# One region of nested arms per expert in a streamed mixture-of-experts loop

## The chip, the cores and the metric

The kernel runs on one core of a Trainium2 chip. The metric is the device time of one execution in microseconds (us), lower is better. A core has five engines that run their own instruction streams and meet through semaphores: TensorE (PE in the profile, with its weight loads as PEld), VectorE (DVE), ScalarE (ACT), GpSimd (POOL) and SyncE (SP). A name with a q (PEldq, ACTq) is the sequencer of that engine: it runs branches, register and semaphore instructions and hands the rest on.

## What is computed

The reference is two post-norm layers of a diffusion backbone over 1024 latent tokens and 256 context tokens, model width 1024, float32. Each layer has a mixing half (attention, pooling, a convolution module, one output projection) and then a hierarchical mixture of experts: each token picks one of four groups and the two best of the eight experts in it, and each expert is a SwiGLU of inner width 512. Cut to what matters here:

```python
def expert_block(args):                     # one block of 128 tokens of one expert
    tb, e = args
    xb = h[tb]
    return (jax.nn.silu(xb @ wg[e]) * (xb @ wu[e])) @ wd[e]
ys = lax.map(expert_block, (tok_buf.reshape(nblk, MOE_BLOCK), blk_e))
return jnp.zeros_like(h).at[tok_buf].add(ys.reshape(P, D) * w_buf[:, None])
```

The router decides at run time how many tokens each of the 32 experts of a layer gets. With the routing that these inputs give, over both layers, 37 experts have at most 64 tokens, 17 have 65 to 128, and 10 have more than 128 (nine of these 129 to 256, one 385 to 448).

## The kernel before

**Stages.** In the profiled execution the mixing half of layer 0 runs to 857 us, its experts from 857 to 1652 us, the mixing half of layer 1 to 2386 us, its experts from 2386 to 3145 us, and a final combination to the end.

**The loop.** `moe` goes over the 32 experts in a Python loop, so each expert has its own code in the program; nothing is reused from one expert to the next. The weights of an expert are 6.29 MB of float32. `e_loads` streams them by SyncE through a ring of 14 units of 1 MiB, six per expert: units 0 to 3 hold gate and up, 4 and 5 the down projection. `load_n` (L2230) reads into registers of every engine the number n of 64-token pieces of an expert, three experts ahead.

**An expert.** `gather` (L2049) fetches up to 128 token rows by an indirect DMA of GpSimd, two experts ahead. `xt_pe` (L2059) transposes them on TensorE in two groups of four, and `xt_copy` brings them to `xT` (ScalarE L2064, VectorE L2065). Then come gate and up:

- `half` (L2092), for at most 64 tokens: 16 matmuls of 64 columns in plain float32 straight from the ring;
- `full`, for more: every product is made of three matmuls of rounded parts (L172 to L174). Weights and tokens must be split first, by `ws` and `xs`: ScalarE makes the high part (`wh`, `xh`, L167), VectorE the rest (`wl`, `xl`, L168). `full` makes the last splits itself; the first, three of weights and two of tokens, are `prep(e)`, made ahead.

`act` (L2140 on ScalarE, L2141 on VectorE) computes silu(gate) times up in two halves `sg`, `ht` (L2147 on TensorE, L2148 on ScalarE) transposes each half into `g`, `down` (L2158) multiplies with the down weights into `mpy`, `evac` (L2163, L2164) copies that to `my`, and `scatter` (L2172) writes the rows out by indirect DMAs.

**The order of an expert.** All of it is written out by hand; each engine runs in program order, and every engine runs every branch. A first nest of `tc.If` (L2264, L2267, L2268) chooses gate and up; then common code follows (the loads, the copies `pl`, the conditional gather `over` of the rows beyond 128 of the expert three ahead, `act`, `xt_pe` of the next expert, `ht`, `xt_copy`); a second nest (L2298, L2301, L2303, L2309) chooses the down projection and, for more than 128 tokens, the second chunk's `act`, `ht` and `down`; then `prep` of the next expert under a branch of its own (L2321), `evac`, loads and `scatter`. The true part of an `If` lies first in the program, its else part behind it, so an expert of over 64 tokens jumps over the code of `half` at L2264, and one of at most 64 tokens jumps, at the end of `half`, over all the code for more. On TensorE this last jump (also L2264) passes 1370 instructions, the one at L2267 1270 and the one at L2298 163.

## Time and profile before

| | us |
|---|---|
| median of 3 runs | 3215.35 |
| lowest, highest | 3204.18, 3216.85 |
| the profiled execution's own time | 3213.33 |
| its span in the trace | 3211.5 |
| experts of layer 0 (857 to 1652 us) | 795 |
| experts of layer 1 (2386 to 3145 us) | 759 |

The profiled execution lies 2 us under the median, and its trace covers all but 1.8 us of it. The change touches only the two expert stages, together 1554 us, so everything is read there. Times in the rows are us unless marked ns. "Idle before" and "waits" name what ended an engine's idle time; "issue" is time in which the engine waited for nothing that the profile shows, as when its sequencer had no instruction to give it. The records of a sequencer's own instructions have a duration too, and for a branch this holds the time until the next instruction is there.

### The profile page before, as it was taken

How to read it: one execution, taken by the hardware profiler on the slowest of the kernel's cores; microseconds unless marked ns; L12 is line 12 of the kernel's file. 1: busy time of each engine (PE TensorE's matmuls, PEld its weight loads, DVE VectorE, ACT ScalarE, POOL GpSimd, SP SyncE). 2: the span in 40 equal slices, each digit the busy share in tenths (PEclk: the TensorE clock that was granted, in tenths of full speed). 3: DMA queues.
4: the chain of work that ended last, by engine and by line, in shares of the span. 5: the costliest groups of instructions: out<-in, count | busy, mean ns of one | idle time of the engine just before them, and what ended most of it. 6: DMA issues, size and time to landing. Idle time of an engine off the chain costs nothing. (4 is left out here: it accounts for less than half of the span.)

```text
span 3211.5 us, 41598 instructions
## 1 busy us (share of the span) xinstructions
PE 2635.0 (82%) x13118; PEld 1663.1 (52%) x13118; DVE 1493.3 (46%) x2851; ACT 1188.0 (37%) x2260; POOL 1070.6 (33%) x919
## 2 busy tenths in 40 slices
PE   6988899998488769879757989999957788798783
PEld 4766565576254435455227766666732344554331
DVE  3355556487543323334149555556851332333215
ACT  3223666632143323333135337665211322333212
POOL 1023999223311121211136349941331111111114
PEclk8998999999799889999878999999978899899997
DMA  7542000042778685757976530002279876645995
GB/s 270 215 142 74 1 1 1 1 158 85 277 297 335 231 310 184 278 188 264 360 295 193 183 136 1 1 1 96 88 260 380 312 288 248 233 158 203 340 361 230
DMA packets 280605, 616.63 MB, mean 192 GB/s; under 512 B 63376, under 2 KB 77072, under 8 KB 271504
## 3 DMA queue, kind: packets, MB, share of 16 engines
q1 hardware_dynamic: 251696, 562.24, 47.9%
q0 software_dynamic: 24544, 37.91, 3.4%
q10 hardware_dynamic: 3712, 8.88, 0.7%
q8 instruction: 275, 4.51, 0.6%
q14 instruction: 378, 3.10, 0.3%
HBM read 577.09 MB, written 73.81 MB: 203 GB/s over the span
## 5 line engine op out<-in xcount | busy, mean ns | idle before, releaser
L1327 DVE TENSOR_REDUCE mx<-S 128x1 f32<-128x1024 f32 (+1 forms) x272 | 215.3, 798 | 208.9 <-PE S L1322 208.5
L172 PE MATMUL gu<-wh,xh 128*128 128x512 f32 x432 | 188.8, 437 | 119.2 <-issue 100.5
L2158 PE MATMUL mpy<-er,g 128*128 128x512 f32 (+1 forms) x672 | 242.8, 630 | 9.9 <-issue 7.3
L2172 POOL DMA_INDIRECT y_d<-my,pl x128 | 140.8, 1100 | 321.5 <-ACTq L2264 108.8
L1339 ACT ACTIVATE P<-S,nb 128x256 f32<-128x256 f32 (+1 forms) x272 | 208.6, 773 | 33.7 <-DVE nb L1331 32.6
L1353 ACT ACTIVATE PT<-pt 128x512 f32<-128x512 f32 (+1 forms) x321 | 169.3, 532 | 135.5 <-PE pt L1344 126.9
L2141 DVE TENSOR_TENSOR sg<-gu,sg 128x256 f32<-128x256 f32 x152 | 57.6, 420 | 342.5 <-ACT sg L2140 337.5
L2171 POOL MEMSET spacer<- 128x1 f32 x152 | 17.6, 116 | 595.7 <-DMA y_d<-my,pl 330.0
L1344 PE MATMUL pt<-ident,P 128*128 128x128 f32 x1312 | 206.7, 282 | 10.1 <-ACT P L1339 10.0
L1388 PE MATMUL po<-PT,V 128*64 128x256 f32 x1312 | 212.5, 403 | 0.1
L2059 PE MATMUL mtp<-ident,xg 128*128 128x128 f32 x600 | 101.1, 300 | 133.7 <-issue 83.3
L178 POOL TENSOR_TENSOR rs_out<-ln_ve,mhalf 128x1 f32<-128x1 f32 x64 | 58.8, 919 | 444.4 <-DVE ln_ve L197 287.8
L2140 ACT ACTIVATE sg<-gu 128x256 f32<-128x256 f32 x152 | 50.3, 383 | 411.3 <-PE gu L2092 285.3
L173 PE MATMUL gu<-wl,xh 128*128 128x512 f32 x432 | 183.0, 424 | 9.0 <-DVE wl L168 9.0
L1344 PEld LDWEIGHTS pt<-ident,P 128*128 128x128 f32 x1312 | 145.3, 141 | 83.4 <-ACT P L1339 41.5
L174 PE MATMUL gu<-wh,xl 128*128 128x512 f32 x432 | 181.4, 420 | 4.3 <-issue 4.3
L168 DVE TENSOR_TENSOR wl<-er,wh 128x1024 fp32r<-128x1024 f32 x102 | 124.3, 1223 | 108.7 <-ACT wh L167 105.1
L172 PEld LDWEIGHTS gu<-wh,xh 128*128 128x128 f32 x432 | 88.9, 206 | 164.9 <-issue 140.2
L2164 DVE COPY my<-mpy 128x512 f32<-128x512 f32 x75 | 51.7, 690 | 260.0 <-PE mpy L2158 252.1
L1321 PE MATMUL S<-KH,Q 128*128 128x512 f32 (+1 forms) x400 | 168.8, 423 | 1.5 <-ACT P L1339 1.5
L2059 PEld LDWEIGHTS mtp<-ident,xg 128*128 128x128 f32 x600 | 77.8, 155 | 173.8 <-issue 125.2
L2092 PE MATMUL gu<-er,xT 128*64 128x512 f32 x720 | 161.4, 594 | 3.2 <-DVEq L2264 2.3
(381 smaller groups left out, 6410.1 us busy)
## 6 DMA issues: line engine op xcount, KB each, us to landing
er<-in_w_e_down SPq DMA_DIRECT2D x66, 1024.0 KB
er<-in_w_e_gate SPq DMA_DIRECT2D x130, 512.0 KB
er<-in_w_e_up SPq DMA_DIRECT2D x130, 512.0 KB
raw<-in_w_mod SPq DMA_DIRECT2D x40, 1024.0 KB
es<-in_w_e_gate SPq DMA_DIRECT2D x64, 512.0 KB
es<-in_w_e_up SPq DMA_DIRECT2D x64, 512.0 KB
es<-in_w_e_down SPq DMA_DIRECT2D x32, 1024.0 KB
raw<-in_w_e_gate SPq DMA_DIRECT2D x40, 512.0 KB
```

The lines of the kernel that those rows point to most:

```text
L172: t.matmul(ps, lh, rh, start=start, stop=False)
L173: t.matmul(ps, lh, rl, start=False, stop=False)
L174: t.matmul(ps, ll, rh, start=False, stop=stop)
L1321: tens.matmul(x[:, c:c + w], q, self.KH[:, g, o:o + w], start=True, stop=False)
L1327: v.tensor_reduce(S[st, "mx"][:, ci:ci + 1], S[st, ci][:, 0:cs[ci][1]], axis=AX.X, op=OP.max)
L1339: act.activation(P[st][:, c:c + w], S[st, ci][:, :w], AF.Exp, bias=S[st, "nb"], accum_out=SU[pi][:, i, h, ci:ci + 1])
L1344: tens.transpose(tp[:, j, :], P[st][:, (g_ * 4 + j) * 128:(g_ * 4 + j + 1) * 128], self.ident)
L1353: act.activation(d, TP[st, g_][:, :m, :], AF.Copy)
L1388: tens.matmul(PO[key][o * 64:o * 64 + 64, :], self.V[:, k0(pi) + j, hp // 2, :], PT[pi, 2 * hp + o][:, j, :], start=(j == 0), stop=(j == n ...
L2059: nc.tensor.transpose(tp[:, j, :], x[:, k * 128:(k + 1) * 128], self.ident)
L2092: nc.tensor.matmul(ps[0][64 * o:64 * o + 64, :], x[:, k, 0:64], w[:, :, o * 256:(o + 1) * 256], start=(k == 0), stop=(k == KD - 1))
L2158: nc.tensor.matmul(py[o][64 * o:64 * o + 64, :] if hf else py[o], g[:, k % 2, z:z + 64] if hf else g[:, k, :], self.unit(e, 4 + k // 2)[:, ...
```

## The change

The two nests become one region per expert. First comes n > 2 (over 128 tokens, `chunks`); its else part, reached by a jump, holds the choice between `small` (at most 64) and `one_chunk`. Each of the three arms holds everything from gate and up to the down projection. In `small` and `one_chunk`, and in `chunks` for its own rare branch, an instruction for every engine's sequencer, made by `mark_branch_hint_location`, announces a coming branch as likely taken: at the start of `small` and `one_chunk` it names the n > 2 branch of the next expert, after gate and up in `chunks` the branch to the code for more than 256 tokens, which now stands at the end of the arm. `preferred_fallthrough_block=True` fixes which part lies directly behind the branch.

Beyond this, `small` computes `act` and `ht` for one half only (the other half is not used in the 64-token form); `follow` copies the next expert's tokens and makes the early split `prep` in the arm, ahead of the down projection and without asking whether the next expert has over 64 tokens; `over` gathers without a branch; the loads of an expert are issued once, behind the region; `prep(0)` loses its branch.

```diff
+HINTED = [mybir.EngineType.PE, mybir.EngineType.Activation, mybir.EngineType.DVE, mybir.EngineType.Pool, mybir.EngineType.SP]
...
-            with tc.If(N[0] > 1):
-                prep(0)
+            prep(0)
+            tc.mark_branch_hint_location(f"many{l}_0", "LikelyTaken", HINTED)
 
             def over(e):
-                with tc.If(N[e] > 2):
-                    gather(xg[2 + e % 3], self.idx_g[:, 1, e:e + 1])
+
+                gather(xg[2 + e % 3], self.idx_g[:, 1, e:e + 1])
...
+            def follow(x, nxt):
+
+                if nxt:
+                    xt_copy(x, nxt)
+                    prep(nxt)
+
+            def small(e, nxt):
+
+                ps, g = GU[e % 2], G[e % 2]
+                hint("many", nxt)
+                half(ps, e)
+                s0 = act(ps, 0)
+                x = tokens(nxt)
+                ht(ps, s0, g, 0)
+                follow(x, nxt)
+                down(g, e, True)
+
+            def middle(ps, g, nxt):
+                s0, s1 = act(ps, 0), act(ps, 1)
+                x = tokens(nxt, (0,))
+                ht(ps, s0, g, 0)
+                x += tokens(nxt, (1,))
+                ht(ps, s1, g, 1)
+                follow(x, nxt)
+
+            def one_chunk(e, nxt):
+
+                ps, g = GU[e % 2], G[e % 2]
+                hint("many", nxt)
+                full(ps, e)
+                middle(ps, g, nxt)
+                down(g, e, False)
+
+            def chunks(e, n, nxt, pl):
+
+                ps, p2, y, y2, g, g2 = GU[e % 2], GU[1 - e % 2], Y[e % 2], Y[1 - e % 2], G[e % 2], G[1 - e % 2]
+                with tc.If(n < 4) as c3:
+                    full(ps, e, xg[2 + e % 3])
+                    half(p2, e)
+                with c3.Else():
+                    double(ps, p2, e)
+                hint("rest", e)
+                middle(ps, g, nxt)
+                down(g, e, False, (0,))
+                s0, s1 = act(p2, 0), act(p2, 1)
...
+                with tc.If(n > 4, label=f"rest{l}_{e}", preferred_fallthrough_block=True):
...
+                with tc.If(n > 2, label=f"many{l}_{e}", preferred_fallthrough_block=True) as c:
+                    chunks(e, n, nxt, pl)
+                with c.Else():
+                    with tc.If(n < 2, preferred_fallthrough_block=True) as c2:
+                        small(e, nxt)
+                    with c2.Else():
+                        one_chunk(e, nxt)
+                self.e_loads(e * 6 + 6 + NU)
+                evac(Y[e % 2])
                 if e + 3 < NE:
                     over(e + 3)
...
-                if nxt:
-                    with tc.If(N[nxt] > 1):
-                        prep(nxt)
```

What this does to the instructions is shown for expert 0 of layer 0, whose gate and up units lie in `raw` and `er`; the numbers are those of buffers. On TensorE before, from the test at L2264 to the start of the down projection for at most 64 tokens (some 400 rows of the other arms lie between the two parts):

```order
L2264 COMPARE_AND_BRANCH
L2092 MATMUL gu_7374<-raw,xT_7397 64x512 x8
L2092 MATMUL gu_7374<-er_7085,xT_7397 64x512 x4
...
L2264 UNCONDITIONAL_BRANCH
...
L2059 MATMUL mtp<-ident,xg_7368 128x128 x4
L2147 MATMUL gu_7374<-ident,sg_7394 128x128 x2
L2059 MATMUL mtp<-ident,xg_7368 128x128 x4
L2147 MATMUL gu_7375<-ident,sg_7395 128x128 x2
L2298 COMPARE_AND_BRANCH
```

TensorE after, the same expert's arm for at most 64 tokens (its test is L2339; `xt_pe` is L2060, the `ht` transposes are L2146, the down projection is L2157):

```order
L2339 COMPARE_AND_BRANCH
L2486 BRANCH_PREFETCH_HINT
L2093 MATMUL gu_7374<-raw,xT_7397 64x512 x8
L2093 MATMUL gu_7374<-er_7085,xT_7397 64x512 x4
...
L2060 MATMUL mtp<-ident,xg_7368 128x128 x8
L2146 MATMUL gu_7374<-ident,sg_7394 128x128 x2
L2157 MATMUL mpy_7378<-er_7087,g_7392 64x512
```

The work of such an expert now lies together, with no branch between gate and up and the down projection; all eight transposes of the next tokens stand ahead of `ht`, and one pair of `ht` transposes is gone.

ScalarE before, the same expert, if it has over 128 tokens: from the next tokens' copy (L2064) over the second chunk's `act` and `ht` to the split for the next expert:

```order
L2064 ACTIVATE xT_7398<-mtp 128x512
...
L2303 COMPARE_AND_BRANCH
L2140 ACTIVATE sg_7394<-gu_7376 128x256
L2140 ACTIVATE sg_7395<-gu_7377 128x256
L2148 ACTIVATE g_7393<-gu_7376 128x256
...
L2321 COMPARE_AND_BRANCH
L167 ACTIVATE wh_7384<-er_7089 128x1024
L167 ACTIVATE xh<-xT_7398 128x512
```

ScalarE after, in the arm for over 128 tokens (`xt_copy` is L2065, `split` L168, `act` L2139, `ht` L2147):

```order
L2065 ACTIVATE xT_7398<-mtp 128x512
L168 ACTIVATE wh_7384<-er_7089 128x1024
L168 ACTIVATE xh<-xT_7398 128x512
L168 ACTIVATE wh_7386<-er_7089 128x1024
L168 ACTIVATE xh<-xT_7398 128x512
L168 ACTIVATE wh_7388<-er_7090 128x1024
L2139 ACTIVATE sg_7394<-gu_7376 128x256
L2139 ACTIVATE sg_7395<-gu_7377 128x256
L2147 ACTIVATE g_7393<-gu_7376 128x256
```

The split of the next expert's weights and tokens has moved from behind the second chunk's `act` and `ht`, where a branch stood ahead of it, to ahead of them.

TensorE before, the end of an expert of over 128 tokens and the next expert's first test (L2264):

```order
L2309 UNCONDITIONAL_BRANCH
L2303 UNCONDITIONAL_BRANCH
...
L2301 UNCONDITIONAL_BRANCH
L2321 COMPARE_AND_BRANCH
...
L2230 TENSOR_LOAD nch
L2264 COMPARE_AND_BRANCH
```

TensorE after, the same end: the test for the rare code (L2319), 112 rows of that code, the jump out of the arm, the arms for fewer tokens, and the next expert's first test (L2336):

```order
L2312 UNCONDITIONAL_BRANCH
L2319 COMPARE_AND_BRANCH
...
L2319 UNCONDITIONAL_BRANCH x2
L2339 COMPARE_AND_BRANCH
...
L2339 UNCONDITIONAL_BRANCH
L2229 TENSOR_LOAD nch
L2336 COMPARE_AND_BRANCH
```

The way out of that arm now leads past the code of the two other arms, 287 instructions on TensorE, and the next n > 2 test has no hint ahead of it on this way. The jump of that test to its else part passes 1153 instructions on TensorE; the jump from the end of `small` to the next test passes 160.

## Rows read from the trace of the kernel before

**Rows 1.** Windows, the two expert stages: engines' busy time (instructions), clock, DMA.

```profile
857.00:1652.00 795.00, 647.32 (x2584) 361.07 (x2584) 266.20 (x420) 249.64 (x401) 142.60 (x192) 0.92 0.75 275
2386.00:3145.00 759.00, 618.91 (x2504) 328.35 (x2504) 213.55 (x364) 204.25 (x352) 126.55 (x189) 0.93 0.77 282
```

The columns are the stretch, its length, then PE, PEld, DVE, ACT and POOL, the granted TensorE clock as a share of full speed, the DMA share and GB/s.

**Rows 2.** Waits of TensorE: what ended them, total us, times, longest.

```profile
PE gu L172 <- issue: 100.5, 14, 14.0
PE mtp L2059 <- issue: 83.3, 28, 7.5
...
PE mtp L2059 <- DVE sg L2141: 18.2, 10, 2.5
...
PE mpy L2158 <- issue: 13.3, 8, 4.6
...
PE gu L2147 <- issue: 4.9, 1, 4.9
```

**Rows 3.** Branch records by line: engine, count, shortest/median/longest ns, first and last start.

```profile
L2264 PEldq COMPARE_BRANCH  x101: 67/217/7411, 860.3 to 3130.9; - x101
L2264 ACTq COMPARE_BRANCH  x101: 34/40/55, 864.5 to 3128.4; - x101
L2267 PEldq COMPARE_BRANCH  x27: 68/6030/8056, 877.3 to 2992.8; - x27
L2298 PEldq COMPARE_BRANCH  x101: 68/211/5717, 872.2 to 3142.2; - x101
```

**Rows 4.** Timeline, expert of at most 64 tokens: start, length, instruction, idle before.

```profile
1596.65 3.60 PE L2092 MATMUL gu<-er,xT 128*64 128x512 f32 x16
...
1600.72 0.76 DVE L2141 TENSOR_TENSOR sg<-gu,sg 128x256 f32<-128x256 f32 x2 [5.60 <-ACT sg L2140]
1602.78 0.63 PE L2059 MATMUL mtp<-ident,xg 128*128 128x128 f32 x4 [2.54 <-issue]
...
1604.21 3.65 PE L2158 MATMUL mpy<-er,g 128*64 128x512 f32 x16
```

**Rows 5.** One branch record each of L2264 (1596) and L2267 (946), TensorE's sequencer.

```profile
L2264 PEldq COMPARE_BRANCH x1: 6181/6181/6181, 1596.0 to 1596.0; - x1
...
L2267 PEldq COMPARE_BRANCH x1: 6475/6475/6475, 946.0 to 946.0; - x1
```

**Rows 6.** Timeline, from such an expert into one of 65 to 128 tokens.

```profile
945.03 1.22 DVE L168 TENSOR_TENSOR wl<-es,wh 128x1024 fp32r<-128x1024 f32 x1
...
952.61 0.77 PE L172 MATMUL gu<-wh,xh 128*128 128x512 f32 x1 [8.22 <-issue]
...
955.98 0.39 PE L174 MATMUL gu<-wh,xl 128*128 128x512 f32 x1
```

**Rows 7.** Windows: two single experts of at most 64 tokens, two runs of them.

```profile
1623.70:1636.40 12.70, 12.19 (x64) 4.65 (x63) 2.35 (x6) 2.51 (x6) 2.31 (x5) 1.00 0.84 295
1607.70:1623.70 16.00, 13.54 (x62) 5.39 (x60) 2.36 (x6) 2.51 (x6) 3.16 (x4) 0.89 1.05 387
...
2400.00:2510.00 110.00, 84.06 (x374) 33.62 (x376) 15.67 (x43) 19.04 (x43) 19.53 (x30) 0.89 1.02 378
3032.00:3142.00 110.00, 92.19 (x437) 39.03 (x438) 16.48 (x42) 18.25 (x44) 20.82 (x35) 0.97 0.99 362
```

**Rows 8.** Groups by form, layer 0's experts: count, busy us, mean ns, idle before.

```profile
L168 DVE TENSOR_TENSOR wl<-er,wh 128x1024 fp32r<-128x1024 f32 x62 | 75.4, 1222 | 59.3 <-ACT wh L167 58.7
...
L167 ACT ACTIVATE wh<-er 128x1024 fp32r<-128x1024 f32 x62 | 65.5, 1058 | 55.3 <-PE gu L174 33.9 <-issue 14.6 <-DMA raw<-in_w_e_up 2.2
...
L2049 POOL DMA_INDIRECT xg<-h_d,idx_g x36 | 42.5, 1181 | 82.1 <-ACT wh L167 22.9 <-DVE pl L2286 22.4 <-issue 12.6
...
L2148 ACT ACTIVATE g<-gu 128x256 f32<-128x256 f32 x76 | 28.5, 384 | 96.8 <-PE gu L2147 96.8
```

**Rows 9.** Timeline, an expert of over 128 tokens: its first down projection.

```profile
1080.14 6.31 PE L2158 MATMUL mpy<-er,g 128*128 128x512 f32 x8 [4.57 <-issue]
```

**Rows 10.** DMA from 3032 to 3142 us, instruction queue: packets, MB, share.

```profile
q8 instruction: 22, 0.36, 1.3%
```

More of the change, by code (lines that the diff above doesn't have):

```diff
@@ L2119, in full, with double @@
                         xt(x, e)
-            def double(ps, p2, e, m):
+            def double(ps, p2, e):
                 prod(ps, 0, 0)
@@ L2255, in moe, with tokens, hint @@
             self.route_rows(sp)
+            def tokens(nxt, hs=range(2)):
+                return xt_pe(xg[nxt % 2], hs) if nxt else []
+            def hint(name, e):
+                if e is not None:
+                    tc.mark_branch_hint_location(f"{name}{l}_{e}", "LikelyTaken", HINTED)
+            def follow(x, nxt):
[11 more added lines that the diff above has]
+                down(g, e, True)
@@ new lines, in middle @@
+            def middle(ps, g, nxt):
[22 more added lines that the diff above has]
+                s0, s1 = act(p2, 0), act(p2, 1)
+                ht(p2, s0, g2, 0)
+                ht(p2, s1, g2, 1)
+                down(g, e, False, (1,))
+                evac(y2)
+                with tc.If(n < 4) as c4:
+                    down(g2, e, True)
+                with c4.Else():
+                    down(g2, e, False)
+                scatter(y2, places(e, 0))
+                for o, z in enumerate(places(e, 1)):
+                    nc.vector.tensor_copy(pl[:, o:o + 1], z)
+                with tc.If(n > 4, label=f"rest{l}_{e}", preferred_fallthrough_block=True):
+                    evac(y)
+                    scatter(y, places(e, 1))
+                    gather(xg[2 + e % 3], self.idx_g[:, 2, e:e + 1])
+                    more(e, n, 2, p2, g2)
+                    nc.vector.memset(pl, OOB)
```

58 lines of the change are left out of this document (1 added, 57 removed).

## The prediction

> **What bounds the kernel now.** I read the windows of the two expert stages first [rows 1]: together 1554 us, in which TensorE is busy for 647.3 + 618.9 = 1266 us, VectorE for 480, and the DMA share is 0.75 and 0.77. TensorE is the fullest engine, yet idle for 288 us, at a granted clock of 0.92 to 0.93. The waits of TensorE say where [rows 2]: 100.5 us ahead of the first product of `full` (14 times), 83.3 us ahead of the next tokens' transposes (28 times), both "issue", so no engine or DMA was waited for. The branch records name the cause [rows 3]: a branch takes ScalarE 40 ns, TensorE mostly 0.2 us, but up to 7.4, 8.1 and 5.7 us at L2264, L2267 and L2298. Two places show it. At 1596.0 the jump out of `half` takes 6.18 us [rows 5]; the 16 matmuls already handed on cover 3.6 us of it, VectorE has finished `sg` by 1601.5, and TensorE starts the transposes at 1602.78 after 2.54 us idle [rows 4]. At 946.0 a jump to an arm of 65 to 128 tokens takes 6.48 us; its first splits are there by 946.3, and the products start at 952.61 after 8.22 us idle [rows 5, 6]. A far jump stalls TensorE's sequencer for about 6.2 us, and what is queued ahead of it (about 3.6 us) hides a part.
>
> The DMA is a second limit close by. In runs of experts with at most 64 tokens its share is 1.02 and 0.99 at 378 and 362 GB/s [rows 7]; 6.29 MB at these rates is 16.6 to 17.4 us per expert, and the last of such experts, with its weights in the ring, needs 12.7 us [rows 7].
>
> **What the change removes.** (1) Into `full`: the arm is entered over one jump, n > 2, hinted a whole arm earlier (12.7 us or more [rows 7]), and the near test L2339. If the hint brings the code, 14 waits of 7.2 us [rows 2] shrink to what a near branch and a late split leave; I keep 1.5 us for each: 14 × 5.7 = **−79**. (2) No jump lies between `half` and the transposes: 28 waits, 83.3 us [rows 2]; I keep 0.4 us each, −72. (3) The same stall stands under other names: "DVE sg" 18.2 us (VectorE's end is only the last event; the longest, 2.5 us, is the size of the wait in [rows 4]), "mpy, issue" 13.3, "gu L2147, issue" 4.9 [rows 2]: 36.4, **−36**. (4) In 37 experts one pair of `ht` transposes and its `act` and copy go. Of the chain from gate and up to the down projection (four transposes 0.63 us, a pair 0.38, a copy 0.38 [rows 4, 8]) about 0.5 us lies on TensorE's path, as the one copy left is no longer hidden behind a second pair: 37 × 0.5 = **−18**, bounds 0 and −37. (5) The clock: an expert that follows a stall runs at 0.89 where another has 1.00 (13.54 against 12.19 us busy [rows 7]), and a product takes 0.77 us just after a stall and 0.39 soon behind [rows 6]. If 1266 us busy went from 0.925 to 0.965, that is 1266 × 0.04 = 51; waits at the DMA's limit will remain, so I take **−30**, bounds 0 and −55.
>
> **What it adds.** (6) The way out of an arm of over 128 tokens: an unhinted jump over 287 instructions, then the unhinted n > 2 test, 1153 instructions to its else part. The shorter jump I price at 3.6 to 4 us (half a far one and more), the far one at 6.2 [rows 5]; the down projection's 3.65 us [rows 4] cover part: about 6.5 us. By the routing, eight of the ten such experts are followed by one of at most 128 tokens: 8 × 6.5 = **+52**, bounds +20 and +80. (7) In that arm ScalarE and VectorE now split for the next expert ahead of the second chunk's `act`: VectorE 3 × 1.22 + 2 × 0.6 = 4.9 us, ScalarE 3 × 1.06 + 2 × 0.5 = 4.2 us [rows 8]. TensorE has the first half of the down projection meanwhile, 8 products of 0.39 us [rows 6], some 3.2 us; then it needs the second `sg`. Today that place already waits 4.57 us for a jump [rows 9], counted in (3). About 3 us left, ten times: **+30**, bounds 0 and +50.
>
> **Costed at nothing.** The early split for next experts of at most 64 tokens: 4.9 us of VectorE beside 3.65 us of down projection and 7.2 us (2 × 3.6 [rows 4]) of the next gate and up; VectorE is busy for 480 of 1554 us. But `evac` is queued behind it on both engines, and the next down projection needs `mpy` free: that comes behind those 7.2 us, so the cover is enough; without it 4.9 − 3.65, some 1.2 us each. `over` now gathers for 54 more experts, 1.18 us of GpSimd each [rows 8], on an engine busy for 269 of 1554 us; their indices are out of bounds, so no rows move. `scatter` is behind it and has until the buffer returns, an expert later. The hints (64 per engine) run in sequencers that are ahead of their engines: 0 to 13 us, at 0.2 us each [rows 3]; I take 0. A hint names the else part, so for ten experts of over 128 tokens it is wrong: 0 to 6.2 us each, 0 to 62; since the block behind the branch is the next in order, I take 0. The loads go out once per expert, but SP waits there for the release of each unit as before: 0. With less time per expert the DMA's limit comes in: 0 to 15 us in the runs of [rows 7].
>
> **Sum.** −79 − 72 − 36 − 18 − 30 + 52 + 30 = −153; 3213.3 − 153 = **3060 us** for the profiled execution, 2 us below the median, so I leave it. Its own range, with the bounds above, is 2985 to 3125.
>
> **Rivals.**
> A, the forecast: hints work on TensorE. For it: each is placed 13 us or more ahead of its branch, and the stall is code loading, not work. Chance 0.55.
>
> B, the hint does nothing. Then each expert of at most 128 tokens still pays the jump at n > 2, now with 3.65 us of down projection queued ahead. But there is one far jump where up to three stood. Of (1) half goes, −40, since the second far jump, L2267, is gone; (2) and (3) change place but not size, 0; (4) −18, (5) −10, (6) +40, as the exit's far jump is then no worse than others: −28, **3185**. Against it speaks nothing in the trace, which shows no hint. Chance 0.15. [...]
>
> C, the fetches themselves become the limit. From 3032 to 3142 us there are 22 instruction fetches [rows 10] for about seven experts, 3.1 each. Fetches run one after another, and one takes about 5.7 us (the records of 3.6 to 6.5 us are one or parts of two): 17.1 us per expert, against 16.6 now. If hinted fetches queue behind the sequential ones, (2) and (3) return as lateness: +12 (0.5 us for each of 23 experts that follow another of at most 64 tokens) − 79 − 10 + 82 = +5, about **3218**, no change. For it: the numbers are that close. Against it: far fewer instructions lie between the parts, so fewer blocks are touched. Chance 0.17.
>
> D, slower: the hinted block is fetched and lost again before the jump, because the arm's own next block is fetched behind it and takes its place. Then each of 54 experts with at most 128 tokens pays the whole 6.2 us of the jump plus 3.6 us of a wasted fetch in the way, less 3.65 queued: 6.15 × 54 = 332 us, against today's 100.5 + 83.3 + 36.4 = 220. 3213 − 18 + 82 + 112 = **3389**. It decides from 3.4 us left per expert on, (220 + 18 + 30 − 82) / 54: above that the kernel is slower. Chance 0.08. The other 0.05 I leave for what I don't see.
>
> **How the numbers follow.** The likeliest is A, 3060. Its own low end, 2985, is the low end of the range; upward the range takes in B at 3185 and the larger part of C, to 3220, which leaves out D, some of C and the tails of A: about 2 in 10. A measurement can tell about 0.5%, 16 us: faster is below 3199, slower above 3231. Faster: A but for its tail, B for the most part, a quarter of C: 0.74. Same: most of C, a little of B: 0.14. Slower: D, a little of C and the unseen: 0.12.
>
> **What would show it.** In the profile after, TensorE's branch records at the n > 2 line (L2336): near 0.2 us for (1) and A, 6 us for B or D, between for C. The waits "issue" ahead of the first product of `full` (100.5 now) and of the transposes (83.3 now) should fall to 20 and 11 us; if the second falls and a wait ahead of gate and up appears, the stall moved rather than went. An expert of at most 64 tokens should take 13 to 13.5 us where the weights are there, 16.6 in long runs, where the DMA's share stays at 1. Behind arms of over 128 tokens 6 to 8 us gaps show (6), a wait of TensorE for `sg` in them shows (7). The granted clock of the expert stages should be about 0.96. The instruction queue's packets separate B and C (as many per expert as now, or more) from A (fewer). Most likely to be wrong is the size of the DMA's limit: in runs of small experts, weights at 16.6 us each leave (2) and (3) less than I count, since time gained on TensorE is lost waiting for weights.

## The result: slower by 1.2%, and the profile after

| | before | after |
|---|---|---|
| median, us | 3212.64 (4 runs) | 3248.05 (4 runs) |
| ratio, 95% interval | | 1.0119 [1.0074, 1.0163] |
| span of the profiled execution | 3211.5 | 3246.7 |

The forecast was 3060 us, its range 2985 to 3220: the change lost 35 us where 153 were to be gained. The line numbers of the changed kernel are one or so off: 173 to 175 the three products of `full`, 2060 the next tokens' transposes, 2093 `half`, 2139 and 2140 `act`, 2146 and 2147 `ht`, 2157 `down`, 2336 the n > 2 test, 2339 the test between the two smaller arms.

The expert stages, in the columns of [rows 1]:

```profile
857.00:1668.00 811.00, 653.93 (x2544) 358.47 (x2544) 335.06 (x485) 300.88 (x448) 171.12 (x219) 0.91 0.73 269
2398.00:3181.00 783.00, 628.41 (x2456) 323.07 (x2454) 303.58 (x452) 272.76 (x422) 164.19 (x224) 0.91 0.75 274
```

They last 811 and 783 us, not 795 and 759. The granted clock, to be 0.96, is 0.91. TensorE's waits, as [rows 2]:

```profile
PE gu L173 <- issue: 109.2, 13, 20.1
PE gu L2146 <- DVE sg L2140: 48.7, 18, 4.5
...
PE mpy L2157 <- ACT g L2147: 17.5, 37, 0.5
```

The wait ahead of the transposes (83.3 us before) is gone from the list, that ahead of the first product of `full` is not (100.5 before). The wait between `act` and `ht` has grown from this row of the kernel before, whose longest was 1.0 us:

```profile
PE gu L2147 <- DVE sg L2141: 14.3, 28, 1.0
```

The last row of the changed kernel is the one copy that nothing hides any more, 0.47 us in each of 37 experts. The branch records, as [rows 3]:

```profile
L2336 PEldq COMPARE_BRANCH  x64: 75/4190/7539, 855.9 to 3159.0; - x64
...
L2336 ACTq COMPARE_BRANCH  x64: 46/54/68, 861.0 to 3162.2; - x64
...
L2339 PEldq COMPARE_BRANCH  x91: 72/226/6832, 856.4 to 3171.2; - x91
```

The forecast wanted 0.2 us at L2336; the median is 4.19. Three single records of it, behind an arm of 65 to 128 tokens, behind one of at most 64, and behind one of over 128:

```profile
L2336 PEldq COMPARE_BRANCH  x1: 354/354/354, 3040.3 to 3040.3; - x1
...
L2336 PEldq COMPARE_BRANCH  x1: 5459/5459/5459, 3088.0 to 3088.0; - x1
...
L2336 PEldq COMPARE_BRANCH  x1: 5677/5677/5677, 1089.5 to 1089.5; - x1
```

They stand for the whole: of the jumps taken there, 13 of 14 behind arms of 65 to 128 tokens take 0.33 to 0.37 us, all 30 behind arms of at most 64 take 2.1 to 5.9 (median 5.2), and the eight behind arms of over 128, where no hint stands, 5.7 to 7.5. The test L2339, which the forecast called near, takes 5.5 to 6.8 us in six of the 17 ways into an arm of 65 to 128 tokens, and 0.23 in the others. "Short" below means under 0.6 us.

Where the time went is best seen per expert, from the start of its first gate and up product to that of the next expert (to its last down product for the last of a layer), read from the timelines of the two kernels and summed by the expert's size and that of the next:

| expert (number) | before, us | after, us |
|---|---|---|
| over 128 tokens (10) | 447.9 | 575.6 |
| 65 to 128 (17) | 400.7 | 375.4 |
| at most 64, next at most 64 (23) | 381.4 | 387.0 |
| at most 64, next 65 to 128 (7) | 171.4 | 145.7 |
| at most 64, next over 128 (5) | 113.6 | 72.7 |
| at most 64, last of a layer (2) | 27.8 | 25.3 |

So −92 us lie with the small experts before bigger ones and with those of 65 to 128 tokens, nothing came in the runs of small ones, and +128 in ten experts. TensorE's idle time, read from the same timelines, says why the third row did not fall: inside those 23 experts it went from 69.9 to 20.8 us, and ahead of the next expert's first product from 5.5 to 55.6. That is the sign that the prediction had named for a stall that moved rather than went. A small expert of such a run (columns as [rows 4]):

```profile
3084.94 1.09 PE L2060 MATMUL mtp<-ident,xg 128*128 128x128 f32 x8
...
3086.06 0.44 PE L2146 MATMUL gu<-ident,sg 128*128 128x128 f32 x2
...
3086.97 3.65 PE L2157 MATMUL mpy<-er,g 128*64 128x512 f32 x16 [0.47 <-ACT g L2147]
...
3093.97 2.83 PE L2093 MATMUL gu<-er,xT 128*64 128x512 f32 x6 [3.35 <-DMA er<-in_w_e_gate]
```

The stall of 2.54 us in the middle [rows 4] is gone; 3.35 us stand at the end instead. The row puts them to a DMA, but the jump record that began at 3088.0 ended at 3093.47, half a microsecond ahead of the product. And the second half of an expert of over 128 tokens, ending in its successor's first product:

```profile
1074.84 0.65 ACT L2139 ACTIVATE sg<-gu 128x256 f32<-128x256 f32 x2
...
1077.14 1.11 PE L2146 MATMUL gu<-ident,sg 128*128 128x128 f32 x4 [3.46 <-DVE sg L2140]
...
1095.80 0.77 PE L173 MATMUL gu<-wh,xh 128*128 128x512 f32 x1 [7.49 <-issue]
```

### The profile page after: what moved, and what is told of

It is laid out like the page before. It is cut to its first block, busy times and chain, and to the rows that moved or that the text cites. A ratio compares the mean times of both kernels' runs of the same rounds, so it can differ in the third digit from the quotient of the medians.

```text
span 3246.7 us, 40308 instructions
## 1 busy us (share of the span) xinstructions
PE 2646.3 (82%) x13044; PEld 1649.1 (51%) x13044; DVE 1649.0 (51%) x3003; ACT 1306.6 (40%) x2372; POOL 1135.6 (35%) x977
## 5 line engine op out<-in xcount | busy, mean ns | idle before, releaser
L2050 POOL DMA_INDIRECT xg<-h_d,idx_g x129 | 149.2, 1157 | 552.0 <-PE gu L175 81.7
L169 DVE TENSOR_TENSOR wl<-er,wh 128x1024 fp32r<-128x1024 f32 x163 | 198.5, 1222 | 157.4 <-ACT wh L168 140.1
L2157 PE MATMUL mpy<-er,g 128*64 128x512 f32 (+1 forms) x672 | 250.5, 641 | 10.1 <-ACT g L2147 9.9
L2140 DVE TENSOR_TENSOR sg<-gu,sg 128x256 f32<-128x256 f32 x115 | 47.7, 423 | 394.3 <-ACT sg L2139 392.9
L2139 ACT ACTIVATE sg<-gu 128x256 f32<-128x256 f32 x115 | 42.8, 383 | 435.6 <-PE gu L2093 335.3
L168 ACT ACTIVATE wh<-er 128x1024 fp32r<-128x1024 f32 x163 | 172.2, 1058 | 110.2 <-PE gu L175 75.9
L1345 PE MATMUL pt<-ident,P 128*128 128x128 f32 x1312 | 206.4, 282 | 11.4 <-ACT P L1340 10.9
L2093 PE MATMUL gu<-er,xT 128*64 128x512 f32 x720 | 175.2, 635 | 47.1 <-DMA raw<-in_w_e_gate 11.2
L174 PE MATMUL gu<-wl,xh 128*128 128x512 f32 x432 | 182.6, 423 | 16.4 <-issue 9.2
L2157 PEld LDWEIGHTS mpy<-er,g 128*64 128x64 f32 (+1 forms) x672 | 90.6, 175 | 133.5 <-issue 112.0
L1220 POOL TENSOR_TENSOR Y<-Y 128x1310 f32<-128x1310 f32 (+1 forms) x60 | 150.7, 2512 | 5.0
```

What stands on the lines that cost most here:

```text
L168: self.nc.scalar.activation(h, src, AF.Copy)
L169: (eng or self.nc.vector).tensor_tensor(l, src, f32(h), op=OP.subtract)
L174: t.matmul(ps, lh, rl, start=False, stop=False)
L1345: tens.transpose(tp[:, j, :], P[st][:, (g_ * 4 + j) * 128:(g_ * 4 + j + 1) * 128], self.ident)
L2093: nc.tensor.matmul(ps[0][64 * o:64 * o + 64, :], x[:, k, 0:64], w[:, :, o * 256:(o + 1) * 256], start=(k == 0), stop=(k == KD - 1))
L2157: nc.tensor.matmul(py[o][64 * o:64 * o + 64, :] if hf else py[o], g[:, k % 2, z:z + 64] if hf else g[:, k, :], self.unit(e, 4 + k // 2)[:, ...
```

## Experiments

Times are medians, with the ratio to the kernel before, run on the same chip, and its 95% interval. "Records" are those of TensorE's sequencer at the expert's hinted first branch, where it is taken.

**1. No hints.** Both calls of `mark_branch_hint_location` are taken out.

```diff
-            tc.mark_branch_hint_location(f"many{l}_0", "LikelyTaken", HINTED)
...
-                if e is not None:
-                    tc.mark_branch_hint_location(f"{name}{l}_{e}", "LikelyTaken", HINTED)
+                pass
```

> The changed kernel without any of its hints; all else stays. Theory (hints work on the way out of arms of 65 to 128 tokens and into the rare code's jump, nowhere else): in the profile after, TensorE's branch record at the n > 2 line is 0.33 to 0.37 us in 13 of 14 jumps behind an arm of 65 to 128 tokens, and 2.1 to 5.9 us in all jumps behind an arm of at most 64. Without hints the 13 pay about 5.4 us, less what is queued, some 2.5 us each, and the ten jumps over the rare code as much: 13 x 2.5 + 10 x 2.5, about +55 us against the changed kernel's 3248, so 3290 to 3320. Rival (hints do nothing, the short records have another reason): 3243 to 3253.

3357.3 us, 1.0446 [1.0416, 1.0477]: the hints are worth 109 us (105 by the two ratios), twice what I expected. The records (all 64, and the instruction queue's line of this kernel's page):

```profile
L2334 PEldq COMPARE_BRANCH  x64: 73/6484/7754, 863.7 to 3264.9; - x64
```

```profile
q8 instruction: 283, 4.64, 0.6%
```

and that line of the changed kernel's page:

```profile
q8 instruction: 236, 3.87, 0.5%
```

None of the 14 records behind 65 to 128 tokens is short now (median 6.6). What I had not expected: those behind at most 64 tokens rise too, from 5.2 to 6.65, and such an expert before another goes from 16.8 to 19.0 us. There are 47 more fetches of 16.4 KB. In the fetch times of the runs of small experts I count three per expert without hints and two with them; without them, one begins some 1 to 3 us after the jump, and the one that ends the stall some 4 us after it. So behind a small arm the hint does not bring the code in time (in the changed kernel a transfer of instructions begins inside 28 of these 30 jumps, a median 2.8 us after their start), but the jump is 1.5 us shorter with it, and there is one fetch less; what the extra one brings was not shown.

**2. The early split put late** in the arm of over 128 tokens, behind the second chunk's `act` and `ht`.

```diff
-                follow(x, nxt)
+                return x                       # middle; one_chunk calls follow itself
...
-                middle(ps, g, nxt)
+                x = middle(ps, g, nxt)
+                if nxt:
+                    xt_copy(x, nxt)
                 down(g, e, False, (0,))
...
+                if nxt:
+                    prep(nxt)
                 with tc.If(n > 4, label=f"rest{l}_{e}", preferred_fallthrough_block=True):
```

> The changed kernel, with the early split of the next expert in the arm of over 128 tokens put back behind the second chunk's act and ht (ahead of the rare code's test); the other two arms as they are. Theory (ScalarE and VectorE are busy with that split when the second chunk's act should start): the ten waits of 3.5 us in that arm go, and some 2 us each of lower clock behind them: -35 to -55, so 3195 to 3215. Rival (the wait is code loading, or the split's time only moves to the next expert's first product): 3240 to 3255.

3197.6 us, 0.9948 [0.9932, 0.9963]. TensorE's program is the same, instruction for instruction, so nothing else can differ there. The ten experts fall from 575.6 to 519.3 us, and their waits:

```profile
PE gu L173 <- issue: 91.5, 10, 20.6
...
PE gu L2146 <- DVE sg L2140: 13.4, 7, 4.9
```

from 48.7 to 13.4 us. That is the price of the early split there: 50 of the 188 us between forecast and result; the two kernels moved in 14 to 17 lie 56.6 us apart. Without it the change is a small gain, at this place of the code.

**3 and 4. A hint on the way out** of that arm, ahead of its last down projection, alone and with experiment 2.

```diff
                 with tc.If(n < 4) as c4:
+                    hint("many", nxt)
                     down(g2, e, True)
                 with c4.Else():
+                    hint("many", nxt)
                     down(g2, e, False)
```

> The changed kernel, with a hint of the next expert's n > 2 branch also in the arm of over 128 tokens, ahead of its last down projection. Theory (behind that arm the n > 2 jump has no hint and costs 5.7 to 7.5 us, which shows as gaps of about 8 us): eight gaps shrink to about 2 us and the clock behind them recovers: -45 to -65, so 3183 to 3203. Rival (a hint some 10 us ahead of its jump comes to nothing, as behind the arms of at most 64 tokens): 3243 to 3253, with the n > 2 records there still at 5 us or more.

> Both edits at once: the split put late in the arm of over 128 tokens, and the hint of the next n > 2 branch in it. Theory (two separate losses): their sum, -80 to -120, so 3128 to 3168, under the kernel before (3213). Rival (each only hides the other, as the late split would lie behind the arm's end once the gap there is gone): the larger of the two alone.

3280.2 us, 1.0198 [1.0164, 1.0232], and 3224.4, 1.0027 [1.0009, 1.0044]: 32 and 27 us worse than without it. The eight records behind that arm fall only from 6.2 to 5.0 and 4.7, as those behind small arms do; in the other arms things became worse: 10 and 11 of 14 short instead of 13. The added instructions move all later code, which experiments 14 to 17 measure; I take no more from these two than that the hint there doesn't remove the stall.

**5 and 6. Lighter weights.** In layer 1 the up weights are left out from the fifteenth ring unit on, in the kernel before and in the changed one; the products use what the ring holds.

```diff
                 for s, nm in enumerate(("w_e_gate", "w_e_up")):
+                    if l == 1 and u >= NU and s == 1:
+                        continue
```

> The kernel before, with the up weights of layer 1 not loaded from the fifteenth ring unit on: 4.2 instead of 6.3 MB per expert there (the products then use what the ring holds). Read: the time from one expert of at most 64 tokens to the next of that kind in layer 1, 16.6 us with all weights. Theory (the DMA at 360 to 380 GB/s and the jump out of gate and up set it about equally): falls to what the jump leaves, 12.7 + 2.5, so 15 to 15.5 us. Rival (weights alone set it): 12.7 to 13.5 us. Other rival (code loading alone): stays at 16 or more.

> The changed kernel with the same weights left out. Read: the same time, 16.8 us with all weights. Theory (code loading sets it: the n > 2 jump behind such an arm still takes 5.2 us, of which 3.65 us of down projection and what is on the way cover a part): 15.5 to 16.5 us, so the change could not shorten runs of such experts whatever the weights do. Rival (weights alone: the jump's stall is gone or covered): 12.7 to 13.5 us.

Whole kernel 3214.3 and 3260.0 us (one run each). The 15 experts of layer 1 that have at most 64 tokens and precede another: before 16.5 with all weights, 16.6 with two thirds; after 16.8 and 16.8. Weights have no part in it, in either kernel: of the three readings "code loading alone" is left, my theory for the kernel before was not right. Nor do the weight transfers lengthen the jumps: the changed kernel's records behind small arms in layer 1 have a median of 5.1 us with all weights and 5.3 with two thirds. The kernel before with lighter weights, from 3032 us on, where all weights gave a share of 0.99 and 362 GB/s [rows 7]:

```profile
3032.00:3142.00 110.00, 81.68 (x365) 32.14 (x367) 14.13 (x36) 15.79 (x38) 17.62 (x31) 0.88 0.62 213
```

0.62 and 213 GB/s, and no faster.

**7 and 8. The hint later in the small arm**, on top of experiment 2: behind gate and up, or behind the next transposes too. A branch that always falls through makes the place.

```diff
-                hint("many", nxt)
                 half(ps, e)
                 s0 = act(ps, 0)               # 7: these two lines inside the If
                 x = tokens(nxt)
-                ht(ps, s0, g, 0)
-                follow(x, nxt)
-                down(g, e, True)
+                with tc.If(n < 2):
+                    hint("many", nxt)
+                    ht(ps, s0, g, 0)
+                    follow(x, nxt)
+                    down(g, e, True)
```

> split_late (3197.6) with the hint in the arm of at most 64 tokens moved behind the 16 gate and up products (a branch that always falls through makes the place). TensorE's sequencer passes it some 3 to 4 us after the arm is entered. Theory (a hint is lost when it comes while the block behind the arm's first one is still being fetched, which lasts to 4 to 6 us after entry): still lost for most, n > 2 records behind these arms stay at 4 to 5 us, time 3190 to 3205. Rival (a hint in that arm is lost for good, whatever its time): 3195 to 3205, all records long. Other rival (its place in the block matters): records fall to 0.35 in most.

> split_late (3197.6) with that hint one step later, behind the next tokens' transposes and ahead of ht, which the sequencer passes some 5 to 6 us after the arm is entered and some 5 us ahead of the n > 2 branch. Theory (the first fetch is over by then): most n > 2 records behind these arms fall to 0.3 to 2.5 us; the weights then limit runs of such experts (16.3 us at 385 GB/s against 16.8 now), and those followed by 65 to 128 tokens gain 2 to 3 us: 3165 to 3190. Rival (the hint there is lost whatever its time): 3193 to 3203 with records at 5 us.

3253.1 us, 1.0129 [1.0083, 1.0176], and 3182.4, 0.9893 [0.9856, 0.9930]. Records behind these arms short in 0 of 30 both times, median 5.1 and 5.2: the time of the hint in the arm makes no difference. In all 30 cases of experiment 8 the last fetch was over when the hint came, by 0.2 to 5.6 us, so "lost while another fetch runs" falls. In 28 of them no transfer of instructions begins between hint and jump; the next begins a median 2.8 us into the jump, where without hints the one that ends the stall begins 4.0 us into it. So the hint is not simply late: it comes a median 5.7 us ahead of the jump (12.1 in the changed kernel, where one or two transfers begin in between), and in those 28 no code comes before the jump. The extra 55 us of the first lie in the small arms (699.9 against 633.1 us, most of it a wait for `sg`, 53.0 us in 35 waits): with a branch ahead of it, `act` starts on ScalarE a median 1.4 us after the last gate and up product, not 0.1. The time of the second is inside the theory's range for another reason than the theory's: the records did not shorten, and the ten arms of over 128 tokens, which the edit doesn't touch, fell by 19.5 us (499.8 against 519.3), more than the whole gain of 15 us over experiment 2; a change of that size can be the place of the code (14 to 17).

**9. The two inner arms swapped**, on top of 2.

```diff
-                    with tc.If(n < 2, preferred_fallthrough_block=True) as c2:
-                        small(e, nxt)
-                    with c2.Else():
-                        one_chunk(e, nxt)
+                    with tc.If(n > 1, preferred_fallthrough_block=True) as c2:
+                        one_chunk(e, nxt)
+                    with c2.Else():
+                        small(e, nxt)
```

> split_late (3197.6) with the two inner arms in the other order: 65 to 128 tokens first, at most 64 last, so that the arm of at most 64 runs straight into the next n > 2 branch and the other jumps over it (some 125 TensorE instructions) at its end. Theory (a hint takes effect only when TensorE's sequencer enters the code block that holds the hinted branch; an arm that jumps there at its end enters it too late): n > 2 records of 0.3 to 0.4 us move from behind arms of 65 to 128 tokens (13 of 14 now) to behind arms of at most 64 (0 of 30 now): fewer than 8 of 14, and 10 or more of 30; time 3180 to 3230. Rival (the length of the arm decides, 20 us against 13): the counts stay 13 and 0. Other rival (a hint is dropped if a fetch runs at its time): the counts stay near 13 and 0 as well.

3246.8 us, 1.0102 [1.0078, 1.0127], worse than I allowed for. Short records: 3 of 14 behind 65 to 128 tokens (13 before the swap), 6 of 30 behind at most 64 (0 before; their median falls from 5.25 to 3.5). Both move as the theory of entry to the branch's code block has it (a block is what one fetch of 16.4 KB brings: from 70 to 823.6 us of the kernel before, where there is no branch, 32 fetches for 8094 matmuls and weight loads, 253 each), and against both rivals, but 6 is short of the 10 I asked for. The swap also does a second thing: the small arm is now reached by another far jump, of the inner test:

```profile
L2343 PEldq COMPARE_BRANCH  x71: 70/233/6961, 863.9 to 3160.1; - x71
```

Its record on the way into a small arm is 0.08 us in experiment 2 and has a median of 5.25 here, 121 us over the 37. That is why the small experts before small ones rise from 388.7 to 442.8 us although more records are short, and since those arms are now entered by this jump, the shift of the counts fits the theory but is not shown to come from the order of the arms alone.

**10 and 12. The nest turned**, on top of 2: small arm last and next to the following branch, with all weights and with the lighter ones.

```diff
-                with tc.If(n > 2, label=f"many{l}_{e}", preferred_fallthrough_block=True) as c:
-                    chunks(e, n, nxt, pl)
-                with c.Else():
-                    with tc.If(n < 2, preferred_fallthrough_block=True) as c2:
-                        small(e, nxt)
-                    with c2.Else():
+                with tc.If(n > 1, label=f"many{l}_{e}", preferred_fallthrough_block=True) as c:
+                    with tc.If(n > 2, preferred_fallthrough_block=True) as c2:
+                        chunks(e, n, nxt, pl)
+                    with c2.Else():
                         one_chunk(e, nxt)
+                with c.Else():
+                    small(e, nxt)
```

> split_late with the nest turned: the hinted outer branch is n > 1, its else part is the arm of at most 64 tokens, which lies last and next to the following expert's branch (130 TensorE instructions, about half a block); over 128 and 65 to 128 tokens are told apart inside, without a hint. Theory (hints act on entry to the branch's block, and here that is the arm's own block in half of the cases): most records of the outer branch behind arms of at most 64 are 0.3 to 0.4 us, the time of such an expert before another falls from 16.9 to the weights' limit, 16.0 to 16.5 us; arms of 65 to 128 tokens now pay an unhinted far jump, 14 to 17 times 2 to 3 us more: total 3195 to 3245. Rival (hints in short arms never act): records at 5 us, the time stays at 16.8 or more.

> small_last with the up weights of layer 1 not loaded from the fifteenth ring unit on. Read in layer 1: an expert of at most 64 tokens before another. Theory (with the code there in time, the weights are what is left): 13 to 14 us, where the same cut left the kernel before and the changed kernel at 16.6 and 16.8. Rival (something else than code and weights sets it): 16 us or more.

3133.4 us, 0.9757 [0.9739, 0.9776]: faster than both kernels, and than I expected. Not for my reason, though: only 3 of 23 records behind small arms are short (median 4.8). Its wait ahead of `full` and its share of the DMA in a run of small experts:

```profile
PE gu L173 <- issue: 53.2, 9, 14.1
```

```profile
2411.00:2453.00 42.00, 36.62 (x176) 14.61 (x174) 19.70 (x30) 16.95 (x28) 13.53 (x18) 1.00 1.02 370
```

The former is half of the changed kernel's. A small expert takes 13.5 us before one of over 128 (14.9 in experiment 2), 17.3 before one of 65 to 128 (20.6) and 15.8 before another small one (16.9); the ten big experts take 498.5 us (519.3), those of 65 to 128 tokens 10 us more together. With lighter weights a small expert before a small one falls in layer 1 from 15.9 to 14.3 us, but in layer 0, where nothing was left out, from 15.7 to 14.8 as well: one run each, so that the weights are part of the limit here is likely, by some 0.7 us each, and not shown. The lighter run took 3105.8 us in all.

**11. Hints for TensorE alone**, on top of 2.

```diff
-HINTED = [mybir.EngineType.PE, mybir.EngineType.Activation, mybir.EngineType.DVE, mybir.EngineType.Pool, mybir.EngineType.SP]
+HINTED = [mybir.EngineType.PE]
```

> split_late (3197.6) with the hints given to TensorE's sequencer alone. Theory (only TensorE's branch records hold stalls, the other engines' are 0.03 to 0.1 us): 3192 to 3203. Rival (the other engines' hints hide part of it, since their programs jump too): 3210 to 3240.

3197.8 us, 0.9949 [0.9932, 0.9965], the same as 3197.6: the other engines' hints make no difference.

**13. The big arm last**, on top of 2, without the n > 2 hints.

```diff
+                with tc.If(n < 3, preferred_fallthrough_block=True) as c:
+                    with tc.If(n < 2, preferred_fallthrough_block=True) as c2:
+                        small(e, nxt)
+                    with c2.Else():
+                        one_chunk(e, nxt)
+                with c.Else():
+                    chunks(e, n, nxt, pl)
```

> split_late with the nest turned the other way: the arm of over 128 tokens lies last, next to the following expert's first test (n < 3, no hint), so its way out is short, and the two common arms leave by a far jump over it, which no hint can name. Theory (the way out of that arm costs about 7 us more each than before): the ten experts of over 128 tokens fall from 519 to 440 to 460 us together, and the 54 others pay a far jump of some 6.6 us at their end, of which 3.65 is covered: those of at most 64 before another from 16.9 to 17.5 to 19 us; total 3200 to 3270. Rival (something else in that arm is slow): they stay above 490.

3261.1 us, 1.0149 [1.0124, 1.0175]. The ten big experts take 464.0 us, near the 440 to 460 expected and near the 447.9 of before; with it the 71 us that experiment 2 left there are 55 us the way out. Of the 16 us that remain, 7.1 are a wait that stands in the changed kernel and in all its variants, in the one expert of over 256 tokens: the gather of its third chunk, issued in `double` before, now stands in the rare code, right ahead of its use.

```diff
-                if m > 4:
-                    gather(xg[2 + e % 3], self.idx_g[:, 2, e:e + 1])
...
+                    scatter(y, places(e, 1))
+                    gather(xg[2 + e % 3], self.idx_g[:, 2, e:e + 1])
+                    more(e, n, 2, p2, g2)
```

In the changed kernel it is the third of TensorE's waits for gathered rows, at 2907 us; before there were two, of 14.1 and 15.2 us, one at the start of each layer's experts:

```profile
PE mtp L2060 <- DMA xg<-h_d,idx_g: 35.9, 3, 14.7
```

The others pay: 65 to 128 tokens 419.1 (374.1), small before small 17.9 us (16.9), small before big 23.9 (14.9).

**14 to 17. The place of the code.** 80 more hint instructions at the start of TensorE's program move all that follows; done to experiment 2, to the changed kernel, to experiment 10 and to the kernel before (its first test gets a label for it).

```diff
+            for _ in range(80 if l == 0 else 0):
+                tc.mark_branch_hint_location(f"many{l}_0", "LikelyTaken", [mybir.EngineType.PE])
```

> split_late (3197.6) with 80 more instructions for TensorE's sequencer at the program's start (the same hint again), which move all its later code by 5 KB, 0.31 of a 16.4 KB fetch, and cost some 3 us. Theory (where an arm is cut by a block's end decides single jumps, but over 64 experts, whose code begins at eight different places in a block, it evens out): n > 2 records behind arms of 65 to 128 tokens short in 11 to 14 of 14, behind arms of at most 64 in 0 to 3 of 30, time 3185 to 3215. Rival (the counts 13 and 0 are the luck of this layout): counts nearer to one another, 8 or fewer of 14 or 8 or more of 30, and a time more than 20 us off.

> The changed kernel (3248) with the same 80 instructions at the start of TensorE's program. Theory (the change is slower by its arms: the ten experts of over 128 tokens cost 128 us more than before wherever the code lies): 3245 to 3295, those ten experts 560 to 600 us together, slower than the kernel before and the kernel before moved. Rival (the loss is the place of the code, of which pad80 showed 39 us): under 3225, the ten experts under 530.

> small_last (3133) with the same 80 instructions. Theory (the turned nest shortens the way of a short arm): 3125 to 3180, still under both kernels. Rival (its time was the luck of where its code lies): 3190 or more.

> The kernel before with 80 such instructions at the start of TensorE's program. Theory (place alone moves any of these kernels by up to 40 us): 3180 to 3260. Rival (only programs with hinted jumps depend on it): 3208 to 3224.

| kernel | us | moved, us | moved, ratio to before |
|---|---|---|---|
| before | 3212.0 | 3203.0 | 0.9963 [0.9947, 0.9979] |
| changed | 3248.1 | 3293.0 | 1.0252 [1.0223, 1.0282] |
| split late (2) | 3197.6 | 3236.4 | 1.0071 [1.0046, 1.0097] |
| small arm last (10) | 3133.4 | 3142.6 | 0.9793 [0.9754, 0.9832] |

The move is worth −9 to +45 us, more than I had expected of it; the 80 instructions themselves, which stand between 0.8 and 8.1 us of the span, are in it. The ten big experts of the changed kernel take 586.5 us when moved, so its loss isn't the place of its code. In it and in experiment 2 the 13 short records become 10, and the 0 of 30 stay: the two kinds of arm differ at either place, but 10 is under the 11 that I asked for, and 39 us is the change of time that the rival had named. The turned nest keeps its gain at both places, experiment 2 does not.

## Why the prediction was wrong, step by step

**What bounds the kernel:** TensorE's far jumps, read from the branch records, was right, and the price of 6.2 us held (a median of 6.2 behind the changed kernel's arms of over 128 tokens, and of 6.6 and 6.65 behind the others without hints). The "second limit close by" was not one: experiments 5 and 6 take a third of the weights away and nothing moves. The DMA share of 1.0 in those stretches told that the ring was being filled, not that anything waited for it; of the waits of TensorE in [rows 2]'s view, none of the expert stages ends on a transfer of weights for more than 2.3 us.

**(1)** −79 us into bigger experts: small experts before bigger ones lost 66.6 us (25.7 + 40.9) and those of 65 to 128 tokens 25.3. The sum of 92 us is near the forecast by luck. Of the 66.6 us only 36.9 are idle time ahead of the next expert's first product (86.2 us before, 49.3 now); the other 29.7 stood inside the small experts and belong to (2) and (3). With what experts of 65 to 128 tokens lost ahead of bigger ones (15.5 to 6.2), the ways into bigger experts gave 46 us, not 79. Into over 128 tokens there is now no jump at all; into 65 to 128 the jump still takes 4 to 5.4 us behind a small arm, and the test L2339, taken as near, is a far jump of 5.5 us or more in six of 17 entries.

**(2) and (4)** −72 and −18 us: this is the step that failed first. It says that no jump lies between gate and up and the transposes. That is true, and the idle time there went (69.9 to 20.8 us); but the arm now ends in the far jump of the next expert's n > 2 test, and its hint, though 12 us ahead, does not bring the code by then (a median record of 5.2 us, with a transfer that begins inside it in 28 of 30): 3.35 us at 3093.97 for 2.54 us at 1602.78, and 55.6 us for 5.5 over the 23 small experts before small ones, which went from 381.4 to 387.0 us. A chain shortened by half a microsecond (4) gave nothing for the same reason: the next jump sets the end. The sum gave one hint behaviour to all arms, and counted no stall at the end of `small`; the runs show two behaviours, 13 of 14 and 0 of 30.

**(3)** −36 us: where it was the jump in `mpy` it is gone (that wait has no row now); the rest went the way of (2). **(5)** −30 us for the clock: none, the granted clock went from 0.92 and 0.93 to 0.91, and TensorE's idle time in the two stages from 288 to 312 us; in the turned nest, with 226 us idle, it is 0.94 and 0.93.

**(6)** +52 us for the way out of the big arm: at most 71 by experiment 2 (519.3 − 447.9), of which 55 went when that arm was put last and 7 are the wait for the gather, which the sum put at nothing. So it measured 55 to 64, 3 to 12 us over the forecast and inside its bounds of 20 to 80. **(7)** +30 us for the early split there: 56 by the ten experts, 50 by the whole kernel, just at and above its upper bound. The wait was right: about 3 us left for each expert, 3.46 in the row above, and 34 us of idle time inside the ten experts beyond what the late split leaves (53.3 and 19.1). What I had not counted is that TensorE's busy time grew by 22 us too (433.6 us, 411.2 with the split late): from 1074.8 to 1082.0, around that wait, the granted clock is 0.56 (its records hold 1.0 and 0.5 alone, and 0.5 from 1075.7 to 1082.5), and the down projection's products take 1.06 us behind it where they took 0.59 ahead of it. Over the ten experts the granted clock is 0.90, and 0.93 with the split late.

**At nothing:** the four other engines' hints cost nothing (experiment 11: 3197.8 us without them, 3197.6 with them), nor did a hint that names the wrong part: the n > 2 records that fall through take at most 0.09 us. The early split in the other arms and the gathers without a branch were not run by themselves. The rare code's gather, which cost 7 us, was not seen.

Together, in the terms of the table: −92 for the first group, +3 for (2) and (4) among the small experts before small ones and the last ones, and +128 for (6), (7) and the gather, in all +39 us on the 1543 that the experts took before; the medians differ by 35.

**The rivals.** A's premise holds for 13 of the 44 hinted jumps that are taken behind an arm; and its bounds, added up, would have given 2954 to 3156, not 2985 to 3125. B, no effect of hints, is refuted: 109 us. Its price was wrong as well: the kernel without hints is B's case and takes 3357, not 3185; the sum for B leaves out (7), and puts the moved stalls at no more than the old. The 13 records of 0.35 us that become 6.6 without the hint speak against it too. C came nearest in time, and in that the runs of small experts gained nothing; but its own count does not come out: there are two fetches for each such expert in the changed kernel, 11.4 us at its 5.7 each, against the 16.8 that the expert takes, and what shows is the wait for one fetch at the jump (28 of 30). The 5.7 us are not the transfer: the 22 of [rows 10] take some 1.0 us each (1.3% of 16 engines in 110 us). Those 22 do run one after another, but of all 275 of that kernel 13 begin before the one ahead has landed. D did not happen as put: the hinted jumps of the changed kernel take at most 5.9 us, the same jumps without hints a median 6.6.

**What stays open.** Why a hint works behind one arm and not behind the other. Its time in the arm is not it (7, 8: 0 of 30 short at either place); the order of the arms may have a part in it (9: 13 of 14 became 3, 0 of 30 became 6, with the second jump that came with it). My theory that a hint takes effect when the sequencer enters the block of code with the hinted branch fits those three, but in experiment 10 it predicted most records short and 3 of 23 were. The gain of that experiment is therefore measured, at two places of the code, but not explained in its parts.

## To carry to other kernels

Before counting a removed jump as gained, look for the next one that the same work must pass: here a far jump at the end of a short arm stalls as one in its middle did (3.35 us for 2.54), and with a hint that stands 12 us ahead of it its record still has a median of 5.2 us, so count hits in the branch records, arm by arm. Look at what the busy engine waits for behind early work on a helper engine: here the second `sg` stood behind the early split, TensorE waited 3.46 us for it, and the products behind the wait took 1.06 us each where they had taken 0.59. And where a program has far jumps, move its code by a few instructions, in the kernel before as well, before you believe a gain of 1%: here 80 instructions moved the time by up to 45 us.

## What the runs showed of the hardware

A jump over the arm of over 128 tokens (1153 instructions) costs TensorE's sequencer a median of 6.2 to 6.65 us without a hint, where ScalarE, VectorE and GpSimd spend 0.03 to 0.1 us on the same branch (L2334 without hints, L2336 with them). With a hint it costs 0.35 us at best (13 of 14 behind the arms of 65 to 128 tokens); behind the small arms, 0 of 30, the hint still saves some 1.5 us (5.2 for 6.65), and at whichever of three places in the arm it stands the median is 5.1 to 5.25. That 80 instructions at the program's start move these kernels by up to 45 us (1.4%) was not expected; nor that a stretch with a DMA share of 1.0 would run no faster when a third of its weights was dropped (16.6 us per small expert for 16.5, at a share of 0.62 for 0.99).
